# Softmax with a relative-position bias: long row runs per partition and a bias strip built on chip

## The chip, the cores and the metric

The kernel runs on one core of one Trainium2 chip. The metric is the device time in microseconds, as the median of several executions; the profile is of one execution.

## The reference

The input is 2 x 8 heads of a 2112 x 2112 matrix of logits in float32 (batch, head, query, key) and a table of 33 biases for each of the 8 heads. Every logit gets the bias of its relative position, clipped to 16 on both sides; then a softmax runs over the keys.

```python
pos = np.arange(S)
rel = pos[:, None] - pos[None, :]
rel_clipped = np.clip(rel, -max_rel, max_rel) + max_rel
bias = rel_bias[:, rel_clipped].copy()
logits = logits + bias[None, :, :, :]
logits = logits - logits.max(axis=-1, keepdims=True)
exp = np.exp(logits)
return (exp / exp.sum(axis=-1, keepdims=True)).astype(np.float32)
```

A row's bias is one constant (`rel_bias[h, 32]`) far to the left of the diagonal, another (`rel_bias[h, 0]`) far to the right, and a band of 33 values between. The input has 285.5 MB and the output as much. Both kernels leave out the subtraction of the maximum, which doesn't change a softmax.

## The kernel before

All rows of all heads are one list of 33,792 rows, cut into 264 tiles `L` of 128 rows: one row of 2112 elements on each partition. A tile is a contiguous piece of 1056 KB; a partition's part of it is 8448 bytes.

The band is the same for every tile up to a shift. Ahead of the loop the kernel makes templates: it loads the small table (L42) and a copy of it for every partition (`rbB`, L44), extends the rows on VectorE (`e8`, L50 to L59), writes them to memory (`eD`, L61), and reads them back so that each partition starts one element further (`X`, L65, in `load_template`); VectorE reverses each into a template `T` of 160 columns (L73), one per head, and `TP` for tiles in which two heads meet. The staging buffer `X` has four copies, so later template loads wait for earlier copies.

The loop over the tiles does this:

- L110: SyncE loads a tile into one of 20 buffers (`io`, 1056 KB in all for each).
- L136: VectorE adds the template to the band only, 160 columns.
- L143 and L151: ScalarE computes the exponential in two parts, left of the band's end with one constant as its bias, right of it with the other, and sums each part into a slot of `s`. The first part includes the band. Tiles in which two heads meet do this for each half.
- L162 and L163: VectorE adds the two sums and takes the reciprocal.
- L165: VectorE scales the row in place.
- L167: GpSimd stores the tile.

Loads go through SyncE's queue, q1 of the profile, and stores through GpSimd's, q0. A scheduler of the framework puts the instructions of each engine in an order from the program's dependencies; it mixes template loads and tile loads on SyncE's queue at the start: one tile, the write of `eD`, one tile, four template loads, one tile, four template loads, and so on. Within an engine instructions start in that order.

Of the kernel before, what the change touches and what calls it, by code (L numbers as in the profile page):

```python
# [1 line left out]

# [4 lines left out]

FP32 = mybir.dt.float32
EXP = mybir.ActivationFunctionType.Exp  # L10
ADD = mybir.AluOpType.add


@with_exitstack
def kernel(
    ctx: ExitStack,
    tc: tile.TileContext,
    logits: bass.AP,
    rel_bias: bass.AP,
    out: bass.AP,  # L20
):
    nc = tc.nc
    P = 128
    B, H, S, S2 = logits.shape
    assert S == S2
    MR = 16
    W = 2 * MR + 1
    BAND = P + 2 * MR
    EXT = P - 1
    ELEN = 2 * EXT + W  # L30

    logits_f = logits.flatten_outer_dims()
    out_f = out.flatten_outer_dims()
    NR = B * H * S
    assert NR % P == 0
    NT = NR // P

    const = ctx.enter_context(tc.tile_pool(name="const", bufs=1))
    dram = ctx.enter_context(tc.tile_pool(name="dram", bufs=1, space=bass.MemoryType.DRAM))

    rb8 = const.tile([H, W], FP32, tag="rb8")
    nc.sync.dma_start(out=rb8, in_=rel_bias)  # L42
    rbB = const.tile([P, H, W], FP32, tag="rbB")
    nc.sync.dma_start(  # L44
        out=rbB,
        in_=bass.AP(tensor=rel_bias.tensor, offset=rel_bias.offset, ap=[[0, P], [1, H * W]]),
    )

    e8 = const.tile([H, ELEN], FP32, tag="e8")
    nc.vector.tensor_copy(out=e8[:, 0:EXT], in_=rb8[:, 0:1].to_broadcast([H, EXT]))  # L50
    nc.vector.tensor_copy(out=e8[:, EXT : EXT + W], in_=rb8[:, :])  # L51
    nc.vector.tensor_scalar(  # L52
        out=e8[:, 0 : EXT + W],
        in0=e8[:, 0 : EXT + W],
        scalar1=rb8[:, W - 1 : W],
        scalar2=None,
        op0=mybir.AluOpType.subtract,
    )
    nc.vector.memset(e8[:, EXT + W :], 0.0)  # L59
    eD = dram.tile([H, ELEN], FP32, tag="eD")  # L60
    nc.sync.dma_start(out=eD, in_=e8)  # L61

    def load_template(t, p0, np_, h):
        x = const.tile([P, BAND], FP32, tag="X", name="X", bufs=4)
        nc.sync.dma_start(  # L65
            out=x[p0 : p0 + np_],
            in_=bass.AP(
                tensor=eD.tensor,
                offset=eD.offset + h * ELEN,
                ap=[[1, np_], [1, BAND]],  # L70
            ),
        )
        nc.vector.tensor_copy(  # L73
            out=t[p0 : p0 + np_],
            in_=bass.AP(
                tensor=x.tensor,
                offset=x.offset + p0 * list(x.ap[0])[0] + (BAND - 1),
                ap=[[list(x.ap[0])[0], np_], [-1, BAND]],
            ),
        )  # L80

    T = []
    for h in range(H):
        t = const.tile([P, BAND], FP32, tag=f"T{h}", name="T")
        load_template(t, 0, P, h)
        T.append(t)
    TP = []
    for k in range(H // 2):
        t = const.tile([P, BAND], FP32, tag=f"TP{k}", name="TP")
        load_template(t, 0, 64, 2 * k)  # L90
        load_template(t, 64, 64, 2 * k + 1)
        TP.append(t)
    io = ctx.enter_context(tc.tile_pool(name="io", bufs=20))
    small = ctx.enter_context(tc.tile_pool(name="small", bufs=16))

    def rb_at(h, k, p0, p1):
        return rbB[p0:p1, h, k : k + 1]

    for t in range(NT):
        rs = P * t  # L100
        f0 = rs // S
        f1 = (rs + P - 1) // S
        if f0 == f1:
            segs = [(0, P, f0, rs - f0 * S)]
        else:
            split = f1 * S - rs
            segs = [(0, split, f0, rs - f0 * S), (split, P, f1, 0)]

        L = io.tile([P, S], FP32, tag="L")
        nc.sync.dma_start(out=L, in_=logits_f[rs : rs + P, :])  # L110

        def seg_ab(p0, p1, i0):
            n = p1 - p0
            c0 = i0 - MR
            return c0, max(c0, 0), min(i0 + n + MR, S)

        max_slots = 1
        for (p0, p1, f, i0) in segs:
            _, _, b = seg_ab(p0, p1, i0)
            max_slots = max(max_slots, 1 + (b < S))  # L120

        s = None
        if max_slots == 2:
            s = small.tile([P, 2], FP32, tag="s", name="s")
        tot = small.tile([P, 1], FP32, tag="tot")

        for (p0, p1, f, i0) in segs:
            h = f % H
            n = p1 - p0
            c0, a, b = seg_ab(p0, p1, i0)  # L130
            nslots = 1 + (b < S)
            if len(segs) == 1:
                tmpl = T[h]
            else:
                tmpl = TP[(f0 % H) // 2]
            nc.vector.tensor_tensor(  # L136
                out=L[p0:p1, a:b],
                in0=L[p0:p1, a:b],
                in1=tmpl[p0 : p0 + n, a - c0 : b - c0],
                op=ADD,  # L140
            )
            acc0 = s[p0:p1, 0:1] if max_slots == 2 else tot[p0:p1, 0:1]
            nc.scalar.activation(  # L143
                out=L[p0:p1, 0:b],
                in_=L[p0:p1, 0:b],
                func=EXP,
                bias=rb_at(h, W - 1, p0, p1),
                accum_out=acc0,
            )
            if nslots == 2:  # L150
                nc.scalar.activation(  # L151
                    out=L[p0:p1, b:S],
                    in_=L[p0:p1, b:S],
                    func=EXP,
                    bias=rb_at(h, 0, p0, p1),
                    accum_out=s[p0:p1, 1:2],
                )
            elif max_slots == 2:
                nc.vector.memset(s[p0:p1, 1:2], 0.0)  # L159

        if max_slots == 2:
            nc.vector.tensor_tensor(out=tot, in0=s[:, 0:1], in1=s[:, 1:2], op=ADD)  # L162
        nc.vector.reciprocal(out=tot, in_=tot)  # L163

        nc.vector.tensor_scalar_mul(out=L[:], in0=L[:], scalar1=tot[:])  # L165

        nc.gpsimd.dma_start(out=out_f[rs : rs + P, :], in_=L[:])  # L167


# [1 line left out]
_INS = ['logits', 'rel_bias']  # L171
_OUTS = [((2, 8, 2112, 2112), 'float32')]


# [23 lines left out]
```

The softmax here doesn't subtract the row's maximum and nothing guards it: scores larger than these inputs give would overflow.

## Time and profile before

| | |
|---|---|
| median of 10 runs | 1363.21 us (1361.78 to 1364.42) |
| the profiled execution | 1364.34 us, its span 1362.2 us |
| VectorE (DVE) busy | 518.6 us, 38% |
| ScalarE (ACT) busy | 657.6 us, 48% |
| GpSimd (POOL) busy, issuing stores | 140.6 us, 10% |
| moved by DMA | 572.36 MB in 78,030 packets, mean 420 GB/s |
| tile load, issue to landing, median | 40.6 us |
| tile store, issue to landing, median | 13.6 us |

The page cuts the span into 40 slices, and each digit is a busy share in tenths. A group of instructions is named by its line, engine, operation and operands, with count, busy time, mean duration and the idle time of the engine before it. The chain that ended last names, going back from the end, what each step waited for. SPq and POOLq are the queues of SyncE and GpSimd, from which DMAs are issued; the time of issue is not the time of moving the data.

### The profile page before, as it was taken

The page shows a single profiled execution, that of the slowest core. Times are in us where ns is not written, and L with a number is a line of the kernel's source. Part 1 is how long each engine was busy: PE and PEld are TensorE (multiplying, and loading weights), DVE is VectorE, ACT ScalarE, POOL GpSimd, SP SyncE. Part 2 cuts the span into 40 slices and gives each one's busy share as a digit, 9 for nine tenths or more (in the row PEclk, how much of TensorE's full clock was granted, in tenths as well). Part 3 has the DMA queues.
Part 4 walks back from the last instruction along what each step waited for, and adds up shares of the span by engine and source line. Part 5 has one row for each costly group of instructions (what it writes and reads, how often), then busy time and mean ns, then how long its engine had stood idle before and what let it go on. Part 6 is the DMA issues. An engine that isn't in the chain of part 4 may idle for free.

```text
span 1362.2 us, 3994 instructions
## 1 busy us (share of the span) xinstructions
DVE 518.6 (38%) x1084; ACT 657.6 (48%) x1057; POOL 140.6 (10%) x268
## 2 busy tenths in 40 slices
DVE  3434343343334333334343333433433433333432
ACT  3454444544445444454444544445444454444543
POOL 0011011010101111111011010111101101101100
DMA  8999999999999999999999999999999999999996
GB/s 293 412 428 428 427 427 428 428 427 427 428 428 427 427 427 429 427 426 428 428 427 426 427 428 428 427 428 428 427 427 427 428 428 427 427 427 428 428 427 285
DMA packets 78030, 572.36 MB, mean 420 GB/s; under 512 B 8744, under 2 KB 10416, under 8 KB 10416
## 3 DMA queue, kind: packets, MB, share of 16 engines
q1 hardware_dynamic: 39984, 286.62, 50.3%
q0 software_dynamic: 38016, 285.49, 49.7%
q14 instruction: 30, 0.25, 0.0%
HBM read 286.59 MB, written 285.48 MB: 420 GB/s over the span
## 4 chain that ended last, share of the span: by engine, by line
DMA 98%; issue 1%; DVE 0%; ACT 0%; SPq 0%; POOLq 0%; POOL 0%; ACTq 0%; DVEq 0%
DMA L<-in_logits_dram 96%; DMA X<-eD 1%; DMA eD<-e 0%; ACT L L143 0%; SPq L110 0%; DMA rb<-in_rel_bias_dram 0%; DVE L L165 0%; DVE T L73 0%; POOLq L193 0%; DVE tot L162 0%; POOL out_dram L167 0%; ACT L L151 0%; DVE tot L163 0%; DVE L L136 0%; DVE e L52 0%
## 5 line engine op out<-in xcount | busy, mean ns | idle before, releaser
L151 ACT ACTIVATE L<-L,rbB 128x1968 f32<-128x1968 f32 (+31 forms) x256 | 297.0, 1160 | 656.1 <-DMA L<-in_logits_dram 614.0
L165 DVE TENSOR_SCALAR L<-L,tot 128x2112 f32<-128x2112 f32 x264 | 348.4, 1320 | 8.4
L143 ACT ACTIVATE L<-L,rbB 128x144 f32<-128x144 f32 (+33 forms) x272 | 333.3, 1225 | 29.5 <-DVE L L136 24.1
L167 POOL DMA_DIRECT2D out_dram<-L x264 | 140.4, 532 | 1213.3 <-DVE L L165 1060.0
L136 DVE TENSOR_TENSOR L<-L,T 128x160 f32<-128x160 f32 (+1 forms) x256 | 82.9, 324 | 351.1 <-DMA L<-in_logits_dram 324.0
L162 DVE TENSOR_TENSOR tot<-s 128x1 f32<-128x1 f32 x256 | 40.7, 159 | 423.2 <-ACT L L143 422.6
L163 DVE RECIPROCAL tot<-tot 128x1 f32<-128x1 f32 x264 | 43.3, 164 | 26.3 <-ACT L L143 17.7
L143 ACT ACTIVATION_READ_ACCUMULATOR L<-L,rbB 128x1 f32 (+1 forms) x272 | 50.7, 186 | 0.0
L151 ACT ACTIVATION_READ_ACCUMULATOR L<-L,rbB 128x1 f32 (+1 forms) x256 | 47.7, 186 | 0.0
L136 DVE TENSOR_TENSOR L<-L,TP 64x80 f32<-64x80 f32 x16 | 3.8, 237 | 7.2 <-DMA L<-in_logits_dram 6.1
L73 DVE COPY T<-X 128x160 f32<-128x160 f32 x8 | 1.7, 238 | 11.4 <-DMA X<-eD 11.4
L151 ACT ACT_TABLE_LOAD x1 | 1.3, 1283 | 8.6 <-DMA L<-in_logits_dram 8.6
L73 DVE COPY TP<-X 64x160 f32<-64x160 f32 x8 | 1.9, 237 | 5.0 <-DMA X<-eD 4.9
L50 DVE COPY e<-rb 8x127 f32<-8x127 f32 x1 | 0.2, 214 | 1.2 <-DMA rb<-in_rel_bias_dram 1.2
L59 DVE MEMSET e<- 8x127 f32 x1 | 0.2, 164 | 0.8 <-PEq L182 0.8
L159 DVE MEMSET s<- 64x1 f32 x8 | 0.5, 59 | 0.0
L52 DVE TENSOR_SCALAR e<-e,rb 8x160 f32<-8x160 f32 x1 | 0.3, 291 | 0.0
L51 DVE COPY e<-rb 8x33 f32<-8x33 f32 x1 | 0.2, 159 | 0.0
L182 POOL MEMSET const-float32-0.0<- 128x1 f32 x1 | 0.1, 98 | 0.2 <-issue 0.2
L182 POOL MEMSET const-bfloat16-1.0<- 128x1 bf16 x1 | 0.1, 101 | 0.0
L182 POOL MEMSET const-float32-1.0<- 128x1 f32 x1 | 0.1, 98 | 0.0
L182 POOL MEMSET const-uint8-127<- 128x1 uint8 x1 | 0.1, 98 | 0.0
## 6 DMA issues: line engine op xcount, KB each, us to landing
L<-in_logits_dram SPq DMA_DIRECT2D x264, 1056.0 KB, 40.6
out_dram<-L POOLq DMA_DIRECT2D x264, 1056.0 KB, 13.6
X<-eD SPq DMA_DIRECT2D x8, 80.0 KB, 4.0
X<-eD SPq DMA_DIRECT2D x8, 40.0 KB, 7.1
rbB<-in_rel_bias_dram SPq DMA_DIRECT2D x1, 132.0 KB, 4.5
rb<-in_rel_bias_dram SPq DMA_DIRECT2D x1, 1.0 KB
eD<-e SPq DMA_DIRECT2D x1, 9.0 KB
```

Source lines behind the costliest of these rows:

```text
L50: nc.vector.tensor_copy(out=e8[:, 0:EXT], in_=rb8[:, 0:1].to_broadcast([H, EXT]))
L52: nc.vector.tensor_scalar(out=e8[:, 0 : EXT + W], in0=e8[:, 0 : EXT + W], scalar1=rb8[:, W - 1 : W], scalar2=None, op0=mybir.AluOpType.sub ...
L73: nc.vector.tensor_copy(out=t[p0 : p0 + np_], in_=bass.AP(tensor=x.tensor, offset=x.offset + p0 * list(x.ap[0])[0] + (BAND - 1), ap=[[list ...
L136: nc.vector.tensor_tensor(out=L[p0:p1, a:b], in0=L[p0:p1, a:b], in1=tmpl[p0 : p0 + n, a - c0 : b - c0], op=ADD,)
L143: nc.scalar.activation(out=L[p0:p1, 0:b], in_=L[p0:p1, 0:b], func=EXP, bias=rb_at(h, W - 1, p0, p1), accum_out=acc0,)
L151: nc.scalar.activation(out=L[p0:p1, b:S], in_=L[p0:p1, b:S], func=EXP, bias=rb_at(h, 0, p0, p1), accum_out=s[p0:p1, 1:2],)
L159: nc.vector.memset(s[p0:p1, 1:2], 0.0)
L162: nc.vector.tensor_tensor(out=tot, in0=s[:, 0:1], in1=s[:, 1:2], op=ADD)
L163: nc.vector.reciprocal(out=tot, in_=tot)
L165: nc.vector.tensor_scalar_mul(out=L[:], in0=L[:], scalar1=tot[:])
L167: nc.gpsimd.dma_start(out=out_f[rs : rs + P, :], in_=L[:])
L182: nc = _bacc.Bacc("TRN2", target_bir_lowering=False, num_devices=1)
```

## The change

The rows are dealt out anew. A pair of heads of one batch is 4224 rows, and each of the 128 partitions now owns 33 consecutive rows of it (33 x 64 = 2112, so 64 partitions have one head and 64 the next). A tile is a chunk of three rows of each partition: 25,344 contiguous bytes for a partition, 278,784 bytes from one partition to the next. There are 8 such pairs with 11 chunks each. The very first chunk is cut into three chunks of one row, and so is the very last: 92 chunks in all.

As a partition owns a block of 33 rows, the whole bias of its rows, 2112 + 32 columns wide, is one strip `F`, and row j of the block reads it shifted by j. VectorE builds the strip on chip once for each pair of heads (in `bias_rows`), from the table and three masks; the masks come from an index pattern that GpSimd writes. The write to memory, the templates and their loads are gone, and the table is the first transfer, issued by ScalarE.

For a chunk, VectorE adds the strip to all three rows in one operation over 6336 elements; ScalarE computes one exponential per row, with a sum, and without a bias of its own; VectorE takes three reciprocals in one operation and scales row by row. Loads go through GpSimd's queue, but for the first four, which SyncE issues; stores go through SyncE's. There are 7 buffers of three rows instead of 20 of one row.

The same scheduler orders VectorE so that in the steady part the add of chunk n+2 stands between the reciprocal and the scale of chunk n. At the start the adds of all three one-row chunks stand ahead of the first reciprocal. Where the pair changes, the two wide operations that build the strip stand between the scales of the chunks before.

The diff, cut to its core:

```diff
-    eD = dram.tile([H, ELEN], FP32, tag="eD")
-    nc.sync.dma_start(out=eD, in_=e8)
-    def load_template(t, p0, np_, h):
...
-    io = ctx.enter_context(tc.tile_pool(name="io", bufs=20))
+    R = 3
+    FW = S + W - 1
+    io = ctx.enter_context(tc.tile_pool(name="io", bufs=7))
+    chunks = []
+    for k in range(H // 2):
+        for b in range(B):
+            sizes = [R] * (W // R)
+            if not chunks:
+                sizes = [1] * R + sizes[1:]
+            if k == H // 2 - 1 and b == B - 1:
+                sizes = sizes[:-1] + [1] * R
...
+    def rows(t, row, j, r):
+        return bass.AP(tensor=t.tensor, offset=t.offset + (row + j) * S,
+            ap=[[W * S, P], [1, r * S]])
+
+    def load(c, eng):
+        k, row, j, r = c
+        L = io.tile([P, R * S], FP32, tag="L", name="L")
+        eng.dma_start(out=L[:, 0 : r * S], in_=rows(logits, row, j, r))
+        return L
+
+    nc.scalar.dma_start(out=rbB, ...)
+    NPRE = 4
+    pre = [load(c, nc.sync) for c in chunks[:NPRE]]
+    for p0 in (0, NB):
+        nc.gpsimd.iota(qm[p0 : p0 + NB], pattern=[[-1, NB]], base=0, channel_multiplier=1, ...)
+    for m, op in ((eq, ALU.is_equal), (lt, ALU.is_gt), (gt, ALU.is_lt)):
+        nc.vector.tensor_scalar(out=m, in0=qm, scalar1=0.0, scalar2=None, op0=op)
+    nc.vector.tensor_copy(out=rbP[0:NB], in_=rbB[0:NB, :, 0, :])
+    nc.vector.tensor_copy(out=rbP[NB:P], in_=rbB[NB:P, :, 1, :])
+
+    def bias_rows(k):
+        F = fpool.tile([P, FW], FP32, tag="F", name="F")
...
+        nc.vector.tensor_scalar(out=rest, in0=lt, scalar1=low, scalar2=None, op0=ALU.mult)
+        nc.vector.scalar_tensor_tensor(out=rest, in0=gt, scalar=high, in1=rest, ...)
+        nc.vector.tensor_tensor(out=blocks, in0=wide(eq), in1=rev, op=ALU.mult)
+        nc.vector.tensor_tensor(out=blocks, in0=blocks, in1=wide(rest), op=ALU.add)
+        nc.vector.tensor_copy(out=F[:, 0:MR], in_=low.to_broadcast([P, MR]))
+        nc.vector.tensor_copy(out=F[:, FW - MR : FW], in_=high.to_broadcast([P, MR]))
+        return F
...
-        L = io.tile([P, S], FP32, tag="L")
-        nc.sync.dma_start(out=L, in_=logits_f[rs : rs + P, :])
+        L = pre[n] if n < NPRE else load(c, nc.gpsimd)
...
+        nc.vector.tensor_tensor(out=L3, in0=L3, in1=F3, op=ALU.add)
+        tot = small.tile([P, R], FP32, tag="tot", name="tot")
+        for i in range(r):
+            x = L[:, i * S : (i + 1) * S]
+            nc.scalar.activation(out=x, in_=x, func=EXP, accum_out=tot[:, i : i + 1])
+        nc.vector.reciprocal(out=tot[:, 0:r], in_=tot[:, 0:r])
+        for i in range(r):
+            x = L[:, i * S : (i + 1) * S]
+            nc.vector.tensor_scalar_mul(out=x, in0=x, scalar1=tot[:, i : i + 1])
...
-        nc.gpsimd.dma_start(out=out_f[rs : rs + P, :], in_=L[:])
+        nc.sync.dma_start(out=rows(out, row, j, r), in_=L[:, 0 : r * S])
```

## The prediction

> **What bounds the kernel now.** I read the page from the coarse to the fine: busy shares, then the slices, the chain of waits, the stretches of time, the waits of the load queue, and last the groups of instructions.
>
> ```profile
> DVE 518.6 (38%) x1084; ACT 657.6 (48%) x1057; POOL 140.6 (10%) x268
> DMA  8999999999999999999999999999999999999996
> GB/s 293 412 428 428 427 427 428 428 427 427 428 428 427 427 427 429 427 426 428 428 427 426 427 428 428 427 428 428 427 427 427 428 428 427 427 427 428 428 427 285
> DMA packets 78030, 572.36 MB, mean 420 GB/s; under 512 B 8744, under 2 KB 10416, under 8 KB 10416
> ...
> DMA 98%; issue 1%; DVE 0%; ACT 0%; SPq 0%; POOLq 0%; POOL 0%; ACTq 0%; DVEq 0%
> ```
>
> No engine is busy half of the time, the DMA engines are busy in all slices but the ends, and the chain is DMA for 98%. So the time is bytes by rate, plus what is lost at both ends. The stretches (columns: us; DVE, ACT, POOL busy; clock; DMA share; GB/s) give both:
>
> ```profile
> 0.00:40.00 40.00, 13.96 (x41) 15.21 (x24) 2.99 (x9) 1.00 0.86 300
> 40.00:1320.00 1280.00, 491.53 (x1017) 626.81 (x1011) 133.89 (x252) 1.00 1.01 427
> 1320.00:1340.00 20.00, 7.78 (x16) 9.39 (x17) 2.12 (x4) 1.00 0.99 418
> 1340.00:1362.20 22.20, 5.32 (x10) 6.16 (x8) 1.59 (x3) 1.00 0.53 219
> ```
>
> For 1280 us the rate doesn't move: 427.5 GB/s. 572.36 MB at that rate are 1338.9 us; the span is 1362.2, so 23.3 us are lost. In the first 40 us 12.0 MB moved where 17.1 would have: 11.9 us lost. The last two rows lose 0.4 and 10.8 us. The sum closes.
>
> ```profile
> SPq L110 <- DMA L<-in_logits_dram: 1153.3, 252, 4.9
> ```
>
> This is SyncE's own wait: a load is held until an earlier load has landed, not until a buffer is free. With 40.6 us from issue to landing and a tile every 5.06 us (the last four land at 1334.07, 1339.14, 1344.20 and 1349.27), eight loads are under way. Both queues always hold work, so removing vector or scalar work gains nothing here.
>
> The groups give the durations for the new work:
>
> ```profile
> L165 DVE TENSOR_SCALAR L<-L,tot 128x2112 f32<-128x2112 f32 x264 | 348.4, 1320 | 8.4
> L136 DVE TENSOR_TENSOR L<-L,T 128x160 f32<-128x160 f32 x240 | 78.0, 325 | 327.0 <-DMA L<-in_logits_dram 300.9 <-DMA out_dram<-L 26.1
> L162 DVE TENSOR_TENSOR tot<-s 128x1 f32<-128x1 f32 x256 | 40.7, 159 | 423.2 <-ACT L L143 422.6 <-ACT L L151 0.4
> L143 ACT ACTIVATE L<-L,rbB 128x2112 f32<-128x2112 f32 x8 | 16.4, 2054 | 24.1 <-DVE L L136 24.1
> ```
>
> An add costs 159 ns for one element and 325 for 160: 1.04 ns an element. A scale of 2112 is 1.32 us, an exponential of a whole row 2.05 us and 0.19 for its accumulator.
>
> **What the Trainium skill says.** "VectorE: DVE Perf Modes", the formula for an fp32 add: (N+151)/0.96 ns. For N=160 that is 324 ns, the trace has 325; for a chunk of 6336 it is 6.76 us, which I use. "DMA: Bandwidth & Descriptors", "Where 436 GB/s comes from": the ceiling is 435.2 GB/s. The trace is 1.8% below. The same page, "Why small descriptors are slow": a fixed cost of about three cycles per packet (3.5 ns at the page's 850 MHz, an estimate). The trace's packet records agree in size: 1056 B take 45 ns, 8448 B take 319 ns, so 0.0371 ns a byte and about 6 ns fixed; each transfer adds a 9 ns completion record on each of its engines. The same page, "Latency and other measured facts", has a price for distant rows, used under the rivals.
>
> **The change part by part.**
>
> *Long runs.* A transfer had 8 packets of 8448 B per engine; now a chunk of three rows has 8 of 25344 B. Bytes: 264 x 2 x 1.0813 = 570.95 MB, and 0.14 for the bias table; at the old rate 1335.6 us. One packet of 25344 B by the slope is 945 ns against 3 x 319 = 957. Per chunk and engine: 8 x 945 + 9 = 7569 against 3 x (8 x 319 + 9) = 7683, 1.5% less, so 1316 us. Bounds: 1311.9 at the ceiling; above, if the run is cut into 8 KB pieces anyway, only completions go (18 in 7683) and 1332.5 stay. A run of this length isn't in the trace, so I take four fifths of the gain: **1320 us** (432.5 GB/s).
>
> *Start.* Gone: two small loads, the write of eD, sixteen template loads, and their waits on SyncE, which stood before the logit loads at L110. Now SyncE issues four loads without a wait and GpSimd three more: 3 x 1.08 + 4 x 3.24 = 16.2 MB, 37.5 us of work. The first 8 us cost 4.0 us of DMA before (215 GB/s); the first load is issued 0.85 us sooner, so 3.2 remain. Then the first stores must free buffers before the 16.2 MB run out. The bias table landed 4.5 us after issue: at about 5.3. The strip is two copies, some nine small operations at 0.2, and two of 2112 elements at 2.36: done near 12.1. The scale of the first row stands on VectorE behind the adds of all three one-row chunks. If these arrive at full speed it ends near 21; if GpSimd's longer packets take turns with SyncE's short ones, the third row gets a quarter of the rate, lands near 27, and the first store leaves near 33. I take 33. Its buffer is back about ten microseconds later, near 43; the loads and the two first stores last to 3.2+37.5+5 = 45.7, and the next load needs a microsecond or two. Gap: 0 to 15 us (the latter if stores wait for the fourth chunk); I take 2. Start in all: **5.2 us** instead of 11.9. The two index patterns on GpSimd aren't in the trace: 0.1 us each (its memsets) to 5 us; they stand beside the table's landing, and SyncE's 6.5 MB cover 15 us of late GpSimd loads.
>
> *Middle.* VectorE: scales 348.5, adds 86 x 6.76 + 6 x 2.36 = 595, reciprocals 92 x 0.164 = 15, four strips 22: 981 us, up from 519, cost nothing while DMA takes 1320. A chunk needs 6.76+0.17+3.96 = 10.9 us of VectorE against 15.0 us of DMA. ScalarE: 264 x 2.24 = at most 591, down from 658: nothing. Rebuilding the strip between heads delays one add by about 5 us: hidden by the load queue. *New wait:* on VectorE the add of chunk n+2 stands before the scale of chunk n, so a store waits for a load two chunks later. A chunk is held 30 us for that landing, then 6.8 + 4.0 + 0.2: 41 us. With load and store at 15 each and 4 to land (the 80 KB loads took 4.0), a buffer's loop is 79 us; seven buffers give 7 x 15.0 = 105. So loads stay queued. Loads moved to GpSimd's queue and stores to SyncE's: one stream each as before, GpSimd issuing 88 at 0.53 us instead of 264: nothing. If that cover fails, the time grows by a seventh of what the loop exceeds 105 by, per chunk.
>
> *End.* Before, the data ended near 1358 and the span 4.2 us later; 6.9 us were lost in gaps, with stores waiting for late adds. Now the last adds and scales end about 9 us after the last landing, while about 20 us of stores (part of one chunk, one whole, three rows) are still to be moved: DMA stays full. I keep 4.2 and 2.4 for engines that finish unevenly: **6.6 us** instead of 11.2 (bounds 4.2 to 11.2).
>
> *Sum:* 1320 + 0.3 + 5.2 + 6.6 = 1332.1 of span. The profiled execution took 1364.3 for its span of 1362.2; the median of ten runs is 1363.2, 1.0 above the span. So 1333, rounded up to **1334 us** for small gaps.
>
> **The rivals.**
>
> *The run length buys nothing* (cut again, or the rate bound elsewhere). For it: 427.5 is already within 2% of the ceiling. Against: the fixed 6 ns in the packet records. 1332.5 + 0.3 + 5.2 + 6.6 + 1 = 1346.
>
> *Start starves.* Seven coarse buffers instead of twenty; stores wait for the fourth chunk and DMA idles 15 us: 1334 + 13 = 1347.
>
> *VectorE becomes the bound.* Its sum passes about 1350 only if the adds run 1.6 times slower than their formula ((1350-386)/595); at twice, 386 + 1190 + ends 15 = 1591. The 1.04 ns of the trace speak against it.
>
> *Distant rows slow the memory: slower than before.* Place: every packet from 40 us on; the 128 rows of a transfer lie 278,784 B apart instead of 8448. Price: the skill's page gives 207 GB/s per direction at a pitch of 512 KiB and 164 at 2 MiB, 21% less, which here would be 1320/0.79 + 13 = 1684. It decides when the steady rate falls below 423 GB/s (570.95/423 = 1350). Against: the pitch is below the page's harmless row and isn't a power of two. No run here shows it.
>
> **How the numbers follow.** Forecast 0.55 (1326 to 1341); no gain from run length 0.25 (1341 to 1352); start starves 0.07 (1342 to 1356); VectorE 0.05 and memory 0.07, both slower; 0.01 between. A measurement tells 0.2% (2.7 us) from no change: faster 0.86, same 0.02, slower 0.12. The range 1325 to 1356 leaves out the slower cases and some of the fast end.
>
> **What would show it.** Right: about 26,700 packets, middle slices at 432 or more, first 40 us above 370 GB/s, VectorE near 72% and SyncE's stores released by VectorE. Packets near 78,000 with 428: the first rival. Slices below 8 after the first: the second. VectorE above 95%: the third. Full slices below 423: the last. A steady rate outside 423 to 435 breaks the forecast.

## The result and the profile after

The changed kernel takes **1340.07 us** (median of 8 runs, 1338.36 to 1344.38) against 1363.39 of the kernel before on the same chips: ratio 0.9833, interval 0.9824 to 0.9842, so 23.3 us faster. The profiled execution took 1340.61 us for a span of 1338.2. Here are the page's lines for busy shares, slices, packets and the chain of waits of the changed kernel:

```profile
DVE 947.8 (71%) x477; ACT 525.1 (39%) x529; POOL 50.2 (4%) x94
DMA  9999999999999999999999999999999999999998
GB/s 388 392 380 432 435 431 432 434 431 432 434 433 432 431 436 432 431 434 433 429 436 433 428 436 433 430 433 435 430 433 435 430 431 435 433 430 435 434 428 350
DMA packets 26652, 571.19 MB, mean 427 GB/s; under 512 B 2960, under 2 KB 3088, under 8 KB 3088
...
DMA 79%; DVE 10%; issue 8%; another core or an unknown queue 1%; ACT 0%; SPq 0%; POOLq 0%; POOL 0%; ACTq 0%
```

VectorE has nearly doubled its work and the kernel is still bound by DMA. The packets have fallen to a third, the plateau is a step higher, and the second and third slices (33 to 100 us) stay below it: that is new. The chain is DMA only for 79%, because the loads now wait for stores, and on the way from a load to a store it goes through VectorE. GpSimd's own wait shows the first half of this:

```profile
POOL L L65 <- DMA out_dram<-L: 1225.7, 84, 42.7
```

Most of the chain's "issue" belongs to VectorE too: its pieces of 6.63 us (at 153.62 us, for instance) lie inside an add of three rows (153.58 to 160.34). So VectorE's part is nearer 18% than 10%. The stretches of the changed kernel (us; DVE, ACT, POOL busy; clock; DMA share; GB/s):

```profile
0.00:40.00 40.00, 16.34 (x23) 7.45 (x7) 2.28 (x9) 1.00 0.97 395
40.00:120.00 80.00, 77.26 (x34) 45.43 (x45) 5.25 (x6) 1.00 0.97 393
120.00:1320.00 1200.00, 854.20 (x420) 472.20 (x478) 42.63 (x79) 1.00 1.00 432
1320.00:1338.20 18.20, 0.00 (x0) 0.00 (x0) 0.00 (x0) 1.00 0.65 276
```

571.19 MB at the plateau's rate, 432.3 GB/s before rounding, are 1321.3 us. Lost against that rate: 40 x (1 - 395/432.3) = 3.5 us in the first stretch, 80 x (1 - 393/432.3) = 7.3 in the second, and 18.2 x (1 - 276/432.3) = 6.6 in the last. Sum 1338.7, the span is 1338.2. The kernel before was 1338.9 + 11.9 + 11.2. So bytes and rate gave 17.6, the first 40 us 8.4, the end 4.6, and the second stretch took back 7.3: 23.3 of the 24.0 between the spans. Of the 17.6, 2.7 are the 1.17 MB that are no longer moved; the rest is rate.

Where the second stretch loses shows in VectorE's timeline of the changed kernel (start, us, operation; idle time before it and what ended it):

```profile
28.39 2.36 DVE L141 TENSOR_TENSOR L<-L,F 128x2112 f32<-128x2112 f32 x1 [7.74 <-DMA L<-in_logits_dram]
...
42.68 6.76 DVE L141 TENSOR_TENSOR L<-L,F 128x6336 f32<-128x6336 f32 x1 [8.92 <-DMA L<-in_logits_dram]
49.35 1.31 DVE L149 TENSOR_SCALAR L<-L,tot 128x2112 f32<-128x2112 f32 x1
...
63.98 3.78 DVE L149 TENSOR_SCALAR L<-L,tot 128x2112 f32<-128x2112 f32 x3
```

```profile
45.00:50.00 5.00, 5.00 (x2) 0.53 (x1) 1.05 (x2) 1.00 1.03 368
50.00:55.00 5.00, 5.00 (x2) 5.00 (x5) 0.00 (x0) 1.00 0.93 353
65.00:70.00 5.00, 5.00 (x5) 5.00 (x6) 1.65 (x1) 1.00 0.65 157
```

The second fence has three stretches of the same run. The third row arrives at 28.4, as worked out. But the fourth chunk, the first of three rows, arrives only at 42.7, together with the seventh (42.8); these two are the last of the loads that were issued at the start. The scale of the third row stands behind its add and ends at 50.7; the fourth chunk itself is scaled by 67.8. By 66 us the loads run out, and DMA moves 157 GB/s for 5 us.

Those 5 us are 3.2 of the 7.3 that are lost. The first of the three stretches shows that a busy share is not a rate: the engines are busy throughout and move 368 GB/s. Between 40 and 120 us, 115 of 1113 packets of 25,344 bytes took more than 960 ns, up to 2789, where the median is 940; 106 of the 115 were loads on GpSimd's queue. Worked out from the packet records, these long packets cost about 4 us, and idle engines about 3. From 120 to 1300 us only 106 of 20,044 packets took so long. Why these packets are slow stays open; they come with the gap and nearly go with it (5 in x1, 51 in x2).

### The profile page after: what moved, and what is told of

Read it like the earlier page. It is cut to its first block, busy times and chain, and to the rows that moved or that the text cites. A ratio compares the mean times of both kernels' runs of the same rounds, so it can differ in the third digit from the quotient of the medians.

```text
span 1338.2 us, 1678 instructions
## 1 busy us (share of the span) xinstructions
DVE 947.8 (71%) x477; ACT 525.1 (39%) x529; POOL 50.2 (4%) x94
## 2 busy tenths in 40 slices
DMA packets 26652, 571.19 MB, mean 427 GB/s; under 512 B 2960, under 2 KB 3088, under 8 KB 3088
## 4 chain that ended last, share of the span: by engine, by line
DMA 79%; DVE 10%; issue 8%; another core or an unknown queue 1%; ACT 0%; SPq 0%; POOLq 0%; POOL 0%; ACTq 0%
DMA out_dram<-L 45%; DMA L<-in_logits_dram 35%; DVE L L149 6%; DVE L L141 3%; DVE F L121 0%; ACT L L145 0%; SPq L65 0%; DVE tot L146 0%; POOLq L65 0%; POOL L L65 0%; ACTq L176 0%; ACTq L145 0%; POOLq L176 0%
## 5 line engine op out<-in xcount | busy, mean ns | idle before, releaser
L141 DVE TENSOR_TENSOR L<-L,F 128x6336 f32<-128x6336 f32 (+1 forms) x92 | 595.2, 6470 | 362.2 <-DMA L<-in_logits_dram 362.1
L145 ACT ACTIVATE L<-L 128x2112 f32<-128x2112 f32 x264 | 515.3, 1952 | 784.8 <-DVE L L141 780.4
L149 DVE TENSOR_SCALAR L<-L,tot 128x2112 f32<-128x2112 f32 x264 | 332.3, 1315 | 0.0
L65 POOL DMA_DIRECT2D L<-in_logits_dram x88 | 49.6, 564 | 1244.5 <-DMA out_dram<-L 1225.7
L145 ACT ACTIVATION_READ_ACCUMULATOR L<-L 128x1 f32 x264 | 49.2, 186 | 0.0
L146 DVE RECIPROCAL tot<-tot 128x3 f32<-128x3 f32 (+1 forms) x92 | 15.5, 169 | 1.2 <-ACT L L145 1.2
L122 DVE TENSOR_TENSOR F<-F,rest 128x2112 f32<-128x2112 f32 x4 | 9.4, 2338 | 0.0
L121 DVE TENSOR_TENSOR F<-eq,rbP 128x2112 f32<-128x2112 f32 x4 | 9.3, 2337 | 0.0
## 6 DMA issues: line engine op xcount, KB each, us to landing
out_dram<-L SPq DMA_DIRECT2D x86, 3168.0 KB, 36.9
L<-in_logits_dram POOLq DMA_DIRECT2D x85, 3168.0 KB, 27.2
```

The costliest lines, as they stand in the source:

```text
L65: eng.dma_start(out=L[:, 0 : r * S], in_=rows(logits, row, j, r))
L121: nc.vector.tensor_tensor(out=blocks, in0=wide(eq), in1=rev, op=ALU.mult)
L122: nc.vector.tensor_tensor(out=blocks, in0=blocks, in1=wide(rest), op=ALU.add)
L141: nc.vector.tensor_tensor(out=L3, in0=L3, in1=F3, op=ALU.add)
L145: nc.scalar.activation(out=x, in_=x, func=EXP, accum_out=tot[:, i : i + 1])
L146: nc.vector.reciprocal(out=tot[:, 0:r], in_=tot[:, 0:r])
```

## The experiments

All times are medians beside the kernel before on the same chip. The first three ask what the gap at 40 to 120 us is.

| kernel | us | ratio to before, interval |
|---|---|---|
| changed | 1340.1 | 0.9833 (0.9824 to 0.9842) |
| x1 all loads in GpSimd's queue | 1332.7 | 0.9776 (0.9762 to 0.9789) |
| x2 fourth chunk to GpSimd's queue | 1332.8 | 0.9776 (0.9762 to 0.9789) |
| x3 loads SyncE, stores GpSimd | 1334.0 | 0.9786 (0.9772 to 0.9799) |
| x4 first chunk whole | 1331.0 | 0.9764 (0.9750 to 0.9777) |
| y1 runs cut | 1344.7 | 0.9861 (0.9848 to 0.9875) |
| y2 before, start freed | 1359.8 | 0.9971 (0.9960 to 0.9982) |
| y3 last chunk whole | 1337.4 | 0.9809 (0.9795 to 0.9822) |
| y4 one more add of a row | 1342.9 | 0.9849 (0.9836 to 0.9863) |
| z1 x1 with runs cut | 1344.5 | 0.9861 (0.9847 to 0.9874) |
| z2 only whole chunks | 1330.5 | 0.9758 (0.9745 to 0.9771) |
| z3 x1 with last chunk whole | 1331.9 | 0.9770 (0.9757 to 0.9783) |
| z4 add twice | 1555.1 | 1.1406 (1.1390 to 1.1421) |

### x1: all loads in one queue

```diff
-    pre = [load(c, nc.sync) for c in chunks[:NPRE]]
+    pre = [load(c, nc.gpsimd) for c in chunks[:NPRE]]
```

> The changed kernel with its first four loads on GpSimd's queue too, so that all loads are in one queue in their order of use and SyncE has only stores. Theory (in the changed kernel DMA lost 7.2 us between 40 and 120 us because two load queues take turns: the fourth chunk, on SyncE's queue, lands last of seven at 42.7 us, and the first two stores stand behind it in that queue): the three one-row chunks have landed by 12 us, the first store starts near 24 instead of 32, the window 40 to 80 us moves at least 425 GB/s instead of 369, and the median falls by 4 to 7 us to about 1334. Rival (the gap belongs to seven coarse buffers and to VectorE's order, whatever arrives first): the window stays under 390 and the median within 2 us of 1340.

1332.7 us. The same stretch of this run:

```profile
40.00:120.00 80.00, 61.70 (x31) 36.34 (x38) 3.16 (x6) 1.00 1.01 432
```

The gap is gone and so are 7.4 us. The three rows had landed by 12.3 us and been added by 17.4, and the add of the fourth chunk began at 19.9. The first store, however, started at 27.9 and not near 24, since the scheduler put the fourth chunk's add ahead of the first scale.

### x2: three rows on SyncE, the fourth chunk on GpSimd

```diff
-    NPRE = 4
+    NPRE = 3
```

> The changed kernel with only the three one-row chunks on SyncE's queue; the fourth chunk is the first on GpSimd's. The rows still take turns with the long packets, so the third lands near 28 us, but the fourth lands near 15 instead of 42.7 and no store stands behind it. Theory (late fourth chunk): most of the 7.2 us comes back, median near 1336, the window 40 to 80 us above 410 GB/s. If instead the late second and third rows are the cause (first store at 32 us), the window stays near 369 and the median near 1340. Rival (coarse buffers): near 1340 too.

1332.8 us; the stretch 40 to 120 moves 424. VectorE's timeline of this run:

```profile
28.23 2.36 DVE L141 TENSOR_TENSOR L<-L,F 128x2112 f32<-128x2112 f32 x1 [7.73 <-DMA L<-in_logits_dram]
30.51 0.16 DVE L146 RECIPROCAL tot<-tot 128x1 f32<-128x1 f32 x1
30.59 6.74 DVE L141 TENSOR_TENSOR L<-L,F 128x6336 f32<-128x6336 f32 x1
37.24 1.31 DVE L149 TENSOR_SCALAR L<-L,tot 128x2112 f32<-128x2112 f32 x1
```

The third row is as late as in the changed kernel (28.2), and the first scale even ends 6 us later (38.5 against 32.2). Yet the gap shrinks to 80 x (1 - 424/432.3) = 1.5 us. So neither the late rows as such nor the date of the first store made it.

The edit also takes away another thing: in the changed kernel the first two stores stood behind the fourth chunk in SyncE's queue. The loads that GpSimd issues next, one for each buffer that comes back, tell the two apart. In the changed kernel and then in x2:

```profile
45.80 0.53 POOL L65 DMA_DIRECT2D L<-in_logits_dram  x1 [42.69 <-DMA out_dram<-L]
48.26 0.53 POOL L65 DMA_DIRECT2D L<-in_logits_dram  x1 [1.94 <-DMA out_dram<-L]
66.23 1.65 POOL L65 DMA_DIRECT2D L<-in_logits_dram  x1 [17.44 <-DMA out_dram<-L]
```

```profile
45.66 0.53 POOL L65 DMA_DIRECT2D L<-in_logits_dram  x1 [42.05 <-DMA out_dram<-L]
48.17 1.40 POOL L65 DMA_DIRECT2D L<-in_logits_dram  x1 [1.98 <-DVE tot L146]
51.45 0.57 POOL L65 DMA_DIRECT2D L<-in_logits_dram  x1 [1.89 <-DMA out_dram<-L]
```

The first two buffers come back at the same time in both runs (their stores land at 45.2 and 47.7 us in the changed kernel, at 45.1 and 47.6 in x2), so x2 gained nothing there. The third comes back 14.8 us sooner: it holds the third row, whose scale in the changed kernel stands behind the add of the fourth chunk. That chunk landed at 17.7 us in x2. So the gap is the late fourth chunk, with VectorE's order behind it.

### x3: queues as before

```diff
     pre = [load(c, nc.sync) for c in chunks[:NPRE]]
...
-        L = pre[n] if n < NPRE else load(c, nc.gpsimd)
+        L = pre[n] if n < NPRE else load(c, nc.sync)
...
-        nc.sync.dma_start(out=rows(out, row, j, r), in_=L[:, 0 : r * S])
+        nc.gpsimd.dma_start(out=rows(out, row, j, r), in_=L[:, 0 : r * S])
```

> The changed kernel with the queues as in the kernel before: all loads on SyncE, all stores on GpSimd. Theory: which queue carries loads is worth nothing in the steady part (432 GB/s as now), and the start is that of one load queue, so the median is within 2 us of the kernel with all loads on GpSimd, near 1334. Rival (the exchange of queues is part of the gain, because GpSimd's issue is held up beside a VectorE that is busy 71% of the time, or engines finish less evenly): slower than 1342, steady rate under 430, or store issues on GpSimd well above the 0.53 us of the kernel before.

1334.0 us; the stretch 120 to 1300 moves 433 GB/s and GpSimd's issue takes 545 ns. The exchange of queues is no part of the gain in rate. Against x1, which differs from x3 by this exchange alone, x3 is 1.3 us slower and the runs do not overlap; the profiles show it at the end, where x3 loses 8.1 us after 1300 and x1 5.3, and x3 wins a little back before. In this pair, then, loads on GpSimd and stores on SyncE are worth about 1 us.

### x4 and z2: without the one-row chunks

x4 removes the cut of the first chunk, z2 that of the last as well:

```diff
-            if not chunks:
-                sizes = [1] * R + sizes[1:]
-            if k == H // 2 - 1 and b == B - 1:
-                sizes = sizes[:-1] + [1] * R
```

> The changed kernel without the cut of the first chunk into three rows: 90 chunks. The first chunk's add is 6.76 us, its three exponentials 6.5, and its scale stands behind the add of the third chunk; four loads on SyncE take turns with three on GpSimd, all seven of 3168 KB (22.7 MB, 52 us of loads). Theory (start is set by when the first buffer comes back): the first store starts later than 32 us, near 50; but there are 4.9 us more of loads to cover each later, so the loss in the first 120 us is between 8 and 20 us instead of 10.7, median 1338 to 1350. Rival (the cut is of no use, because loads cover it): 1340 or lower.

> The changed kernel without either cut: 88 whole chunks, the queues as in the changed kernel (four loads on SyncE, the rest on GpSimd). Theory (the gap comes from unequal packets in two load queues, so whole chunks have none; the cut of the last chunk is worth nothing because the backlog of stores fills DMA after the last landing): 1329 to 1332, as x4_first_chunk_whole at 1331.0. Rival (the cut of the last chunk does shorten the end, and y3_last_chunk_whole was faster only by the scatter of its gap): 1333 to 1338.

1331.0 and **1330.5 us**: with this pair of load queues the cut at the start costs 9 us instead of gaining some, even though the first store of z2 starts only at 43.2 us. Of z2, the stretches:

```profile
0.00:40.00 40.00, 20.89 (x19) 7.91 (x8) 2.28 (x9) 1.00 0.97 399
40.00:120.00 80.00, 75.55 (x36) 46.92 (x48) 2.90 (x4) 1.00 1.00 430
```

Seven whole chunks are 22.7 MB, 52 us of loads instead of 37.5, and packets of one length let the two queues advance evenly; which of the two closes the gap isn't separated here (y1 below has packets of one length and only 16.2 MB of first loads, and no gap). For x4 my theory (1338 to 1350) failed and the rival held: the time of the first store doesn't set the start as long as enough loads are queued. z2 came as expected. z2 has the lowest median of all versions, ahead of both kernels; its runs overlap with those of x4.

### y1 and z1: what the long run is worth

```diff
-        L = io.tile([P, R * S], FP32, tag="L", name="L")
-        eng.dma_start(out=L[:, 0 : r * S], in_=rows(logits, row, j, r))
+        L = io.tile([P, R, SP], FP32, tag="L", name="L")      # SP = S + 8; the store and the views of rows follow
+        eng.dma_start(out=L[:, 0:r, 0:S], in_=rows(logits, row, j, r))
...
-            ap=[[W * S, P], [1, r * S]],
+            ap=[[W * S, P], [S, r], [1, S]],
```

> The changed kernel with its rows 32 bytes apart in the buffers, so that each transfer of a chunk has three runs of 8448 bytes per partition and not one of 25344; the partitions' rows in memory, the chunks, the queues and the order are the same. Theory (the long run saves two fixed packet costs of three: a chunk's packets take 8 x 940 ns on an engine instead of 24 x 319): 26,600 packets become about 74,000, the steady rate falls from 432 to 427.5 or 428, and the time rises by 11 to 14 us to about 1353. Rival (the rate came from the distant rows, the fewer completions or the exchange of queues): 1340 to 1344, steady rate 431 or more.

1344.7 us, only 4.6 more, where the theory had 11 to 14; the number lies just beyond the rival's range. The packet line of y1's page, and its stretches:

```profile
DMA packets 70683, 571.19 MB, mean 426 GB/s; under 512 B 2960, under 2 KB 3088, under 8 KB 3088
```

```profile
40.00:120.00 80.00, 75.42 (x34) 47.59 (x48) 4.53 (x5) 1.00 1.01 427
120.00:1300.00 1180.00, 836.50 (x408) 465.95 (x470) 92.22 (x78) 1.00 1.01 428
```

The rate fell as the theory said, to 428; but the gap vanished with it, and the rows landed at 7.5, 12.5 and 18.0 us instead of 8.2, 18.3 and 28.4: with packets of one length each queue got half of the rate and not a quarter. The fourth chunk came at 33.2 us. The two effects offset each other. So I cut the runs where there is no gap, in x1:

> All loads in one queue (as in x1_loads_one_queue, 1332.7 us) and the runs cut to 8448 bytes (as in y1_cut_runs, 1344.7 us). Theory (the cut costs the steady rate 432 to 428 and, in the changed kernel, hid behind it that packets of equal length take turns evenly, which removed the gap between 40 and 120 us): without the gap on both sides the cut costs its whole price, 1332.7 + 11 to 14 = 1344 to 1347. Rival (the long run itself is worth only the 4.6 us seen between the changed kernel and y1_cut_runs): about 1337.

1344.5 us against x1's 1332.7: the run length alone is worth **11.8 us** (11.6 by the ratios, since the two ran on different chips). The long stretch of z1 is at 428 as well:

```profile
120.00:1300.00 1180.00, 832.05 (x404) 460.26 (x466) 60.36 (x78) 1.00 1.01 428
```

### y2: the kernel before with its start freed

```diff
-    nc.sync.dma_start(out=rb8, in_=rel_bias)
+    nc.scalar.dma_start(out=rb8, in_=rel_bias)
...
+    pre = []
+    for t in range(8):
+        L = io.tile([P, S], FP32, tag="L", name="L")
+        nc.sync.dma_start(out=L, in_=logits_f[P * t : P * t + P, :])
+        pre.append(L)
...
-    nc.sync.dma_start(out=eD, in_=e8)
+    nc.gpsimd.dma_start(out=eD, in_=e8)
```

(The table copy `rbB` goes to ScalarE's queue and the reads of `X` to GpSimd's likewise.)

> The kernel before with its start freed: the tables are loaded from ScalarE's queue, the writing and reading of templates is on GpSimd's, and SyncE issues tile loads without a template load between them; eight are issued at once. Runs stay at 8448 bytes. Theory (11.9 us were lost in the first 40 us, of which 3.5 are unavoidable): the first 40 us move 380 GB/s or more instead of 300, the time falls by 6 to 9 us to about 1356. Rival (the start was hidden, since what is late there is caught up by 20 buffers): 1362 to 1364.

1359.8 us, 3.7 less: a smaller gain than the theory had, a larger one than the rival's. Its stretches:

```profile
0.00:8.00 8.00, 0.76 (x4) 0.00 (x0) 0.85 (x5) 1.00 0.77 249
8.00:40.00 32.00, 11.72 (x32) 14.90 (x23) 13.73 (x21) 1.00 1.01 402
40.00:80.00 40.00, 22.29 (x52) 28.32 (x45) 6.26 (x12) 1.00 1.01 420
```

The first 40 us moved 14.9 MB instead of 12.0, 6.7 us gained; that is 372 GB/s, and the theory had 380 or more. 0.7 are lost until 80. The rest, some 2 us, was given back at the end: from 1320 us on it lost 13.3 us (24.9 us of work in 38.2) against 11.2. Why the end is longer was not looked into.

### y3 and z3: the last chunk whole

The edit is the last two lines of z2's, in the changed kernel (y3) and in x1 (z3).

> The changed kernel without the cut of the last chunk: 90 chunks. After the last landing: add 6.76, three exponentials 6.4, reciprocal 0.17, three scales 3.9, so the last store starts about 17 us after the landing and moves 3.24 MB in 7.5 us. Theory (in the changed kernel the stores of earlier chunks fill DMA for about 16 us after the last landing, so a last store that starts at 17 us loses little of DMA but its own 7.5 us come later than the 2.5 of one row): slower by 3 to 8 us, 1343 to 1348. Rival (the backlog of stores hides the whole chain): within 2 us of 1340.

> All loads in one queue (as in x1_loads_one_queue, 1332.7 us), the last chunk whole. It prices the cut of the last chunk without the scatter of the gap. Theory (the backlog of stores covers the last chunk's chain): 1330 to 1333. Rival (cut is worth 3 us or more): 1336 or more.

1337.4 and 1331.9 us. y3 came out faster, against the theory; but the kernels with the gap scatter (1338.4 to 1344.4 for the changed one, 1335.7 to 1339.5 for y3), so z3 is the price: 0.8 us less than x1, with overlapping intervals. The cut at the end gains nothing measurable. The backlog of stores shows in z3: the last load lands at 1291.3 us and the last store is issued at 1309.6; DMA moves 431 GB/s from 1291 to 1300, 416 until that issue and 419 from there to 1324.

### y4 and z4: how much vector work is free

```diff
+        if r == R:      # y4; z4 repeats the whole add
+            y = L[:, 0:S]
+            nc.vector.tensor_tensor(out=y, in0=y, in1=F[:, W - 1 - j : W - 1 - j + S], op=ALU.add)
```

> The changed kernel with one more add of 2112 elements on the first row of each three-row chunk (the bias of that row is added twice): 86 x 2.35 = 202 us more of VectorE, from 948 to 1150 us, a chunk 13.1 us of VectorE against 15.0 of DMA. Theory (vector work is covered up to 15.0 us a chunk): the steady rate stays at 432, the start may lose some 3 to 8 us more since VectorE is full from 42 to 120 us, so 1340 to 1350. Rival (VectorE is on the path, as its 10% of the chain of waits could be read): 100 us or more slower.

> The changed kernel with the add of every three-row chunk done twice (the bias is added twice there). VectorE then has 948 + 86 x 6.66 = 1521 us, a chunk 17.5 us of it against 15.0 of DMA. Theory (vector work is free up to 15.0 us a chunk and then sets the time): VectorE busy 97% or more and 1530 to 1560 us. Rival (the waits in VectorE's order, the add of two chunks ahead before the scale, cost more once it is full): above 1600.

1342.9 and 1555.1 us, both where the theory had them. 191 us more of VectorE cost 2.9 us, with overlapping runs; 565 us more cost 215. The busy lines of the pages of y4 and of z4:

```profile
DVE 1138.8 (85%) x563; ACT 529.6 (39%) x529; POOL 52.5 (4%) x94
```

```profile
DVE 1512.6 (97%) x563; ACT 525.2 (34%) x529; POOL 64.1 (4%) x94
...
DMA  9979999999979899999898999999998899999757
```

In y4 the long stretch stays at 432 GB/s; in z4 it falls to 375 and VectorE has taken over. The share of VectorE in the changed kernel's chain is a link of the loop through store and load, not a bound.

## Why the prediction was right, point by point

1334 was forecast with a range of 1325 to 1356, and the forecast's own interval ended at 1341; 1340.1 is inside both. It is also 6.1 us above the forecast, whose gain was 29, and lies midway between the forecast and the second rival's 1347, "start starves", which had a chance of 0.07. So the number is right by its range, and one term is wrong by 5 us (see the start). Of the marks named in advance, packets (26,652), middle slices (432 on average, 428 to 436), VectorE (71%), the first 40 us (395) and the waits of SyncE's stores came as said. The mark against the second rival, slices of the DMA digits below 8, could not catch what happened: the digit stays 9 while the third slice moves 380 GB/s.

*Long runs: right, with some luck.* 1320 was taken for the bytes, 1321.3 came out. The step assumed 945 ns for a packet of 25,344 bytes; the packet records of the changed kernel show 940 against 319 for 8448. z1 prices the edit at 11.8 us; the sum had 15.6 (1335.6 to 1320), of which 3.1 stood for fewer completion records (1335.6 to 1332.5); z1 doesn't bring those back, since its transfers are as many, so 11.8 stand against 12.5. The luck is in the "four fifths". With the measured 940 ns the same sum gives 7529 against 7683 and 1309 us, a gain of 27 us where the rate gave 15. The records of short packets overlap a little: the DMA share of the plateau is 1.01 before and 1.00 after, so part of what a long packet saves had been hidden. The step took too little from the packets (1.5% for 2.0%) and then lowered it, and the two met near the measured 1.1%.

*Start: the term that was mis-sized.* "Gap: 0 to 15 us; I take 2" measured 7.3. The first 40 us were right (3.5 for 3.2), and so were the third row's landing (28.4 for 27) and the first store (32.2 for 33). But these were the wrong marks: x2 has a later first store and next to no gap. The term had the right case at its upper end ("the latter if stores wait for the fourth chunk"), and I put it almost at nothing without working out when that chunk lands. It stands on SyncE's queue behind the rows and landed at 42.7 us, and the scale of the third row and all stores after it wait for its add. The step asked when the first buffer is back, near 43; that came at 45.8, and it was the third that was missing. The table landed at 8.4 us instead of 5.3; in x2 it is as late (8.2) and the gap all but gone, so it is not the cause.

*Middle: right.* VectorE's 981 us came out as 947.8 and cost nothing; y4 shows that 13.1 us a chunk are still covered, z4 that 17.5 are not. The order "add of chunk n+2 before scale of chunk n" is in the chain of waits, and SyncE's stores wait on VectorE, not on a landing:

```profile
SPq L150 <- DVE tot L146: 1204.7, 84, 32.8
```

The buffers' loop nevertheless has room: the rate is the plateau's in every slice from the fourth to the last but one. A chunk's load took 27.2 us from issue to landing and its store 36.9 (medians), where the step had 19 for each, because they stand in line: work is always queued.

*End: right in size.* 6.6 us were forecast and 6.6 measured. VectorE's last scale ends at 1319.7, and DMA still has work for most of the time that is left. That the backlog of stores does it, and not the one-row chunks, is what z3 adds.

*Around the span:* 1.9 us between the span and the median, where 1.0 was taken. Together: 1.0 of rate, 5.3 of gap and 0.3 in the first stretch are 6.6, of which 0.5 is rounding, since the span came out at 1338.2 against 1332.1. The 0.9 around the span is what the forecast had been rounded up by.

*The rivals.* "The run length buys nothing" is out by z1. "Start starves" gave the right place at half its size. VectorE as the bound is real but begins somewhere between 13.1 and 17.5 us of work a chunk (y4, z4). Rows 278,784 bytes apart did not slow the memory: 428 GB/s with short runs at that distance (y1, z1), as the kernel before had at 8448.

## What to carry to other kernels

When DMA sets the time, write the span as bytes by the plateau's rate plus what is lost at both ends, and price every edit in those terms; an edit's effect on the ends can hide its effect on the rate, as in y1, so test each where the other is absent. Read the rate and not only the busy share: engines that were busy throughout moved 368 GB/s. At the start, what has to land early is not the first buffer but the one for which the engine that works in order is waiting: here loads in one queue in their order of use closed the gap (x1, x3), and so did packets of one length (y1). Cutting the first and last chunks finer did not help in any pair of runs: with two load queues whole chunks were 9.6 us faster, and even against x1, which has both cuts and no gap, 2.2.

## What the runs showed of the hardware that was not expected

- From 319 ns for 8448 bytes and 940 ns for 25,344, a packet costs 0.0368 ns a byte and 8.5 ns fixed, more than the 6 ns that the 1056-byte packets suggested; sixteen engines at that slope are 435 GB/s, the ceiling in the Trainium skill's "DMA: Bandwidth & Descriptors", "Where 436 GB/s comes from". The rate shows a smaller fixed part, since records overlap a little: 427.5 and 432.3 GB/s over sixteen engines are 316 and 938 ns a packet, and 5 ns fixed (an estimate from these rates).
- Two queues that both had loads took turns packet by packet: between 12 and 26 us of the changed kernel, 179 packets of 8448 bytes and 179 of 25,344 started. So the rows landed 10.1 us apart (8.2, 18.3, 28.4), a quarter of the rate, and in y1, beside packets of their own length, 5.1 to 5.4 us apart.
- An exponential of a row of 2112 took 1952 ns without the table's value as its bias, and 2054 ns with it in the kernel before: 102 ns.
- GpSimd's issue of a store took 532 ns on average in the kernel before and 1064 ns in y2, with the same stores; it cost nothing visible there. The cause is open.
